# Windowed attention inside a hybrid encoder: the two halves of each P^T V product issued as a pair, transposes ordered by key block over two K heads, a fourth P^T buffer

## The chip, the cores and the metric

One core of a Trainium2 chip runs the whole program. The metric is device time in microseconds (us) of one execution; the median of several executions is compared.

## The reference

A trunk of two layers runs over two sequences, one of 2048 and one of 256 tokens, with 1024 features: first a windowed attention layer, then a bidirectional mLSTM layer, each with RMS norm, a gate, an output projection and a residual. The change touches the attention layer alone. Its core is:

```python
s = jnp.einsum('bnqgrd,bnkgd->bngrqk', qb, kb, preferred_element_type=jnp.float32)
s = s * (ATTN_HEAD_DIM ** -0.5)
...
s = jnp.where(mask[None, :, None, None], s, -jnp.inf)
...
m = jnp.maximum(jnp.max(s, axis=-1, keepdims=True), sk)
p = jnp.exp(s - m)
den = jnp.sum(p, axis=-1, keepdims=True) + jnp.exp(sk - m)
p = (p / den).astype(vb.dtype)
o = jnp.einsum('bngrqk,bnkgd->bnqgrd', p, vb).reshape(B, S, ATTN_WIDTH)
```

There are 16 query heads in 4 groups of 4, one K head (64 wide) to a group. A block of 128 queries looks at its own block of 128 keys and at its two neighbours.

## The kernel before

The tokens are 18 tiles of 128: tiles 0 to 15 are the long sequence, 16 and 17 the short one. `attn_core` (line 394) goes through them. For tile t:

- `front(t + 2)` projects two tiles ahead: three outputs of 512 columns (K and V, and two halves of Q), each 24 products on PE at lines 376 to 378 (`pj`), since an fp32 operand is split into a high and a low part and three of the four cross products are taken. Rotations run on DVE, then `pk` and `pqt` transposes on PE (lines 433, 451), then casts to `KH`, `KL`, `Q` on ACT and DVE (lines 435, 436, 454 to 457).
- `scores()` takes the K heads g = 0 to 3 in turn. For each of the 4 query heads of g, two products of 384 columns on PE fill a PSUM tile `s` (lines 500, 501), and DVE adds the mask into an SBUF tile `Sm` with the row maximum on the side (line 503). Then DVE makes `nm` and `es` (lines 508, 510) and ACT takes four exponentials in place (line 514). There are 11 buffers for `Sm` (`NSM`), four of them taken by each K head.
- `transposes()` turns the probabilities over. For one K head and one key block j, four PE transposes (line 528) fill a PSUM tile `ptp` (two buffers), and a copy (line 531) takes it to an SBUF tile `PT`: on ACT for j = 0, on DVE for the others. There are 3 buffers for `PT` (`NPT`). K heads go one after the other, each through all its key blocks.
- `values()` takes K heads in pairs P = 0, 1. One PSUM tile `o` (one buffer) holds both heads of a pair, the even one in partitions 0 to 63, the odd one in 64 to 127. For each key block and each of the two heads, one product (line 541, 128 x 64 weights of V, 512 columns of `PT`) adds into its half. An ACT copy (line 544) then takes `o` to `scr`, and a DMA stores it.

A tile at the edge of a sequence (0, 15, 16, 17) has two key blocks, the others three. So there are 800 transposes and 200 products of P^T with V. In the trace each of these products stands as two rows, for it passes its columns twice: 400 rows of line 541.

The order on the engines is set by the framework: the program is recorded with the generators interleaved by the string `AORDER` (f, s, p, v: a step of front, scores, transposes, values), and a scheduler with its own timeline then fixes the order of the instructions on each engine. A buffer is given when its last reader is done. Each engine then runs its list strictly in that order.

After attention come the gate product (`attn_gate`, whose weights `w_z` are loaded and split on ACT and DVE during the last tiles), the output projection and the mLSTM layer; the change does not touch them.

Of the kernel before, what the change touches and what calls it, by code (L numbers as in the profile page):

```python
# [11 lines left out]
F32 = mybir.dt.float32  # L12
# [13 lines left out]
HEADS, KVH, HD = 16, 4, 64  # L26
# [14 lines left out]
WOPS = ("b11", "t2", "b21", "t3", "t1", "t4", "b22")  # L41
PAIRS = [(t, t + 1) for t in range(0, NT, 2)]
NSM = 11
NPT = 3
SPT = 18
AORDER = "fffssssfsffffppsvppv"
AORDER1 = "fffssssfsffffppsvppv"
# [8 lines left out]
def seg_of(t):  # L56
    for s in SEGS:
        if s[0] <= t < s[1]:
            return s


class Trunk:
# [330 lines left out]
    def attn_core(self):  # L393
        nc, tc, a = self.nc, self.tc, self.a
        with ExitStack() as st:
            pe = st.enter_context(tc.tile_pool(name="a1e", bufs=2, reuse_waits="tile"))
            p = st.enter_context(tc.tile_pool(name="a1", bufs=2, reuse_waits="tile"))
# [67 lines left out]
            def half(t, h):  # L465
                X[t] += self.split(self.stage(a["xT"][t][:, h * 512:(h + 1) * 512]), nc.gpsimd if h else nc.vector)
# [12 lines left out]
            def core(t):  # L479
                s0, s1 = seg_of(t)  # L480
                kbs = [b for b in (t - 1, t, t + 1) if s0 <= b < s1]
                sl = sorted(b % 3 for b in kbs)
                vof = {b % 3: Vr[b] for b in kbs}
                nk = len(sl)
                step = sl[1] - sl[0]
                win = slice(sl[0], sl[-1] + 1, step)
                Ss, PTs = {}, {}

                def scores():
                    for g in range(KVH):  # L490
                        mx = p.tile([128, 4], F32, tag="mx", name="mx", bufs=3)
                        Sg = []
                        for c in range(GRP):
                            h = g * GRP + c
                            Q = QS[t, h // 8]
                            q = Q[:, h % 2, (h % 8) // 2, :]
                            spare = NT - 2 <= t < SPT and c % 3 == 2
                            S = (pq if spare else ps).tile([128, 3, 128], F32, tag="tq" if spare else "s", name="s",
                                                           bufs=1 if spare else 2)
                            nc.tensor.matmul(S[:, :nk, :], q, KH[:, g, win, :], start=True, stop=False)  # L500
                            nc.tensor.matmul(S[:, :nk, :], q, KL[:, g, win, :], start=False, stop=True)  # L501
                            Sm = p.tile([128, 3, 128], F32, tag="Sm", name="Sm", bufs=NSM)
                            nc.vector.tensor_tensor_reduce(Sm[:, :nk], S[:, :nk], mask[:, t % 3, win, :], 1.0, MASKED,  # L503
                                                           ALU.add, ALU.max, mx[:, c:c + 1])
                            Sg.append(Sm)
                        hs = slice(g * GRP, (g + 1) * GRP)
                        nm = p.tile([128, 4], F32, tag="nm", name="nm", bufs=3)
                        nc.vector.scalar_tensor_tensor(nm[:], mx[:], -HD ** -0.5, nsink[:, hs], ALU.mult, ALU.min)  # L508
                        es = p.tile([128, 4], F32, tag="es", name="es", bufs=3)
                        nc.vector.tensor_add(es[:], sink[:, hs], nm[:])  # L510
                        nc.scalar.activation(es[:], es[:], AF.Exp)
                        rs = p.tile([128, 4], F32, tag="rs", name="rs", bufs=3)
                        for c in range(GRP):
                            nc.scalar.activation(Sg[c][:, :nk], Sg[c][:, :nk], AF.Exp, bias=nm[:, c:c + 1],  # L514
                                                 scale=HD ** -0.5, accum_out=rs[:, c:c + 1])
                        Ss[g] = Sg
                        yield

                        nc.vector.tensor_add(rs[:], rs[:], es[:])
                        nc.vector.reciprocal(self.den[:, t, g // 2, :, g % 2], rs[:])  # L520

                def transposes():
                    for g in range(KVH):
                        PTs[g] = []
                        for j in range(nk):
                            tp = ps.tile([128, 4, 128], F32, tag="tr", name="ptp", bufs=2)
                            for c in range(GRP):
                                nc.tensor.transpose(tp[:, c, :], Ss[g][c][:, j, :], self.ident[:])  # L528
                            pt = p.tile([128, 512], F32, tag="PT", name="PT", bufs=NPT)
                            eng = nc.scalar.copy if j == 0 else nc.vector.tensor_copy  # L530
                            eng(pt[:], tp[:].rearrange("p c q -> p (c q)"))  # L531
                            PTs[g].append(pt)
                        yield

                def values():
                    for P in range(2):
                        o = ps.tile([128, 512], F32, tag="o", name="o", bufs=1)
                        for j in range(nk):
                            for gg in range(2):
                                g = 2 * P + gg  # L540
                                nc.tensor.matmul(o[gg * 64:(gg + 1) * 64, :], vof[sl[j]][:, g * HD:(g + 1) * HD],  # L541
                                                 PTs[g][j][:], start=j == 0, stop=j == nk - 1)
                        ob = self.scr[:, P * 512:(P + 1) * 512]
                        nc.scalar.copy(ob, o[:])
                        nc.sync.dma_start(self.oT[t][:, P * 512:(P + 1) * 512], ob)
                        yield

                return scores(), transposes(), values()

            def front(t):  # L550
# [555 lines left out]
```

## Time and profile before

| | |
|---|---|
| median of 3 runs | 2333.14 us (2330.55 to 2336.04) |
| profiled execution, its own time | 2326.69 us |
| span of its trace | 2324.8 us |
| TensorE's granted clock, mean over the span | 0.984 |
| PE busy | 2239.7 us, 96% |
| DVE busy | 1564.6 us, 67% |
| ACT busy | 1096.1 us, 47% |
| line 541, products of P^T with V | x400, busy 148.0 us together |
| line 528, transposes to `ptp` | x800, busy 127.9 us together |

PE is the matmul engine, PEld its weight loads, DVE the vector engine, ACT the scalar engine. Times of day in the trace count from the start of the span. A busy time is the union of the instructions in a group, and a mean is the length of one; since matmuls are pipelined, one that follows another starts before the first has ended, so what an instruction costs is read from one start to the next. PEclk is the granted share of the full 2.4 GHz. Attention's tiles run from about 60 to 712 us.

### The profile page before, as it was taken

What the parts mean: (1) busy time and instruction counts of PE and PEld (TensorE: products, weight loads), DVE (VectorE), ACT (ScalarE), POOL (GpSimd) and SP (SyncE); (2) the same over time, 40 slices, a digit from 0 to 9 for tenths busy, and PEclk for the clock granted to TensorE, in tenths of its full rate; (3) what the DMA queues carried; (4) which work ended last, traced back from release to release, by engine and by line L of the source; (5) the groups of instructions that cost most, each with busy time, mean ns of one, the idle gap of its engine ahead of it and who ended that gap; (6) DMA issues with size and microseconds to landing.
All of it is one profiled execution on the core that took longest, in us unless ns stands there. A gap on an engine that the chain in (4) does not pass through costs nothing.

```text
span 2324.8 us, 32958 instructions
## 1 busy us (share of the span) xinstructions
PE 2239.7 (96%) x11102; PEld 1775.3 (76%) x11102; DVE 1564.6 (67%) x3403; ACT 1096.1 (47%) x2503; POOL 461.4 (20%) x392
## 2 busy tenths in 40 slices
PE   8999999999999998999899999999999996999998
PEld 7766666666666886888788899978877875888887
DVE  7575656565877779768655522397888786777784
ACT  6464545454765334445533411256454445554463
POOL 3212121212001221322000000012242234333320
PEclk9999999999999999999999999999999997999999
DMA  7111111111225447657533722354565457656642
GB/s 264 48 38 48 38 48 38 48 38 39 91 64 162 147 159 229 230 195 250 189 114 123 245 92 92 113 177 136 175 211 182 132 181 242 207 191 198 209 163 69
DMA packets 170281, 326.41 MB, mean 140 GB/s; under 512 B 18784, under 2 KB 21632, under 8 KB 170112
## 3 DMA queue, kind: packets, MB, share of 16 engines
q1 hardware_dynamic: 169968, 324.30, 42.0%
q8 instruction: 88, 1.44, 0.3%
q14 instruction: 81, 0.66, 0.1%
q10 hardware_dynamic: 144, 0.01, 0.0%
HBM read 235.34 MB, written 88.89 MB: 139 GB/s over the span
## 4 chain that ended last, share of the span: by engine, by line
PE 78%; DVE 8%; DMA 7%; issue 2%; ACT 2%; POOL 2%; SPq 0%; DVEq 0%; POOLq 0%; ACTq 0%
PE pj L378 9%; PE pj L376 9%; PE pj L377 9%; PE o L541 5%; PE pj L271 4%; PE pj L272 4%; PE pj L273 4%; PE ptp L528 4%; PE d L271 3%; PE d L272 3%; PE d L273 3%; PE c L272 3%; PE c L273 3%; PE c L271 3%; DMA qs<-rows 2%
## 5 line engine op out<-in xcount | busy, mean ns | idle before, releaser
L122 ACT CAST xhi<-rawx 128x512 fp32r<-128x512 f32 x372 | 228.6, 618 | 459.6 <-PE pj L377 109.0
L376 PE MATMUL pj<-whi,xhi 128*128 128x512 f32 (+2 forms) x1152 | 429.9, 374 | 8.5 <-ACT whi L167 6.9
L378 PE MATMUL pj<-whi,xlo 128*128 128x512 f32 (+2 forms) x1152 | 423.8, 373 | 5.8 <-DVE xlo L123 3.9
L377 PE MATMUL pj<-wlo,xhi 128*128 128x512 f32 (+2 forms) x1152 | 425.4, 369 | 0.0
L123 DVE TENSOR_TENSOR xlo<-rawx,xhi 128x512 fp32r<-128x512 f32 x338 | 247.6, 737 | 81.7 <-ACT xhi L122 73.9
L378 PEld LDWEIGHTS pj<-whi,xlo 128*128 128x128 f32 x1152 | 217.3, 189 | 56.1 <-issue 14.6
L376 PEld LDWEIGHTS pj<-whi,xhi 128*128 128x128 f32 x1152 | 217.4, 189 | 48.5 <-ACT whi L167 7.3
L377 PEld LDWEIGHTS pj<-wlo,xhi 128*128 128x128 f32 x1152 | 217.4, 189 | 37.4 <-issue 3.2
L271 PE MATMUL pj<-whi,xhi 128*128 128x512 f32 x480 | 194.3, 405 | 13.9 <-DVE x L612 8.9
L503 DVE CUSTOM_DVE_ANT_0 Sm<-s,mask 128x384 f32<-128x384 f32 (+1 forms) x272 | 137.7, 529 | 92.0 <-PE s L501 90.9
L514 ACT ACTIVATE Sm<-Sm,nm 128x384 f32<-128x384 f32 (+1 forms) x288 | 166.9, 581 | 68.2 <-DVE nm L508 67.0
L272 PE MATMUL pj<-wlo,xhi 128*128 128x512 f32 x480 | 192.7, 401 | 2.9 <-DVE wlo L190 2.9
L273 PE MATMUL pj<-whi,xlo 128*128 128x512 f32 x480 | 191.8, 400 | 0.0
L541 PE MATMUL o<-PT,V 128*64 128x512 f32 x400 | 148.0, 623 | 4.5 <-DVE PT L531 4.1
L528 PEld LDWEIGHTS ptp<-ident,Sm 128*128 128x128 f32 x800 | 94.3, 141 | 64.8 <-issue 31.2
L531 DVE COPY PT<-ptp 128x512 f32<-128x512 f32 x128 | 86.6, 686 | 71.8 <-PE ptp L528 37.7
L528 PE MATMUL ptp<-ident,Sm 128*128 128x128 f32 x800 | 127.9, 280 | 4.1 <-ACT Sm L514 1.7
L271 PE MATMUL d<-whi,xhi 128*128 128x512 f32 x320 | 128.1, 400 | 0.0
L272 PE MATMUL c<-wlo,xhi 128*128 128x512 f32 x320 | 127.2, 398 | 0.0
L273 PE MATMUL c<-whi,xlo 128*128 128x512 f32 x320 | 127.1, 397 | 0.0
L273 PE MATMUL d<-whi,xlo 128*128 128x512 f32 x320 | 127.0, 397 | 0.0
L271 PE MATMUL c<-whi,xhi 128*128 128x512 f32 x320 | 127.0, 397 | 0.0
(243 smaller groups left out, 4714.1 us busy)
## 6 DMA issues: line engine op xcount, KB each, us to landing
rawx<-xn2T SPq DMA_DIRECT2D x144, 256.0 KB, 3.1
x<-x SPq DMA_DIRECT2D x108, 256.0 KB, 3.8
rawx<-xT SPq DMA_DIRECT2D x72, 256.0 KB, 2.9
raww<-w_oz SPq DMA_DIRECT2D x64, 256.0 KB, 4.4
raww<-w_qkvg SPq DMA_DIRECT2D x40, 256.0 KB, 4.0
v<-v SPq DMA_DIRECT2D x18, 516.0 KB, 3.7
rawx<-v SPq DMA_DIRECT2D x36, 258.0 KB, 2.7
rawx<-x SPq DMA_DIRECT2D x36, 256.0 KB, 3.0
```

What stands on the lines that cost most here:

```text
L122: nc.scalar.copy(hi[:], src)
L123: (eng or nc.vector).tensor_sub(lo[:], src, hi[:].bitcast(F32))
L271: nc.tensor.matmul(o, xh, wh, start=i == 0 and not more, stop=False, skip_group_check=more)
L272: nc.tensor.matmul(o, xh, wl, start=False, stop=False, skip_group_check=more)
L273: nc.tensor.matmul(o, xl, wh, start=False, stop=i == 3, skip_group_check=more)
L376: nc.tensor.matmul(o[:, :n], xh, wh, start=kt == 0, stop=False)
L377: nc.tensor.matmul(o[:, :n], xh, wl, start=False, stop=False)
L378: nc.tensor.matmul(o[:, :n], xl, wh, start=False, stop=kt == KT - 1)
L503: nc.vector.tensor_tensor_reduce(Sm[:, :nk], S[:, :nk], mask[:, t % 3, win, :], 1.0, MASKED, ALU.add, ALU.max, mx[:, c:c + 1])
L514: nc.scalar.activation(Sg[c][:, :nk], Sg[c][:, :nk], AF.Exp, bias=nm[:, c:c + 1], scale=HD ** -0.5, accum_out=rs[:, c:c + 1])
L528: nc.tensor.transpose(tp[:, c, :], Ss[g][c][:, j, :], self.ident[:])
L541: nc.tensor.matmul(o[gg * 64:(gg + 1) * 64, :], vof[sl[j]][:, g * HD:(g + 1) * HD], PTs[g][j][:], start=j == 0, stop=j == nk - 1)
```

## The change

`transposes()` now goes pair by pair, key block by key block, and within a key block over both K heads; it yields after the first and after the last key block of a pair. There are four `PT` buffers in place of three. `values()` issues the odd head's product of a key block first and places the even head's right behind it in PE's order: `tc.issue_after` puts the instructions recorded inside it directly behind the one named. No instruction is added or removed.

```diff
-NPT = 3
+NPT = 4
...
                 def transposes():
-                    for g in range(KVH):
-                        PTs[g] = []
-                        for j in range(nk):
+                    for P, j in product(range(2), range(nk)):
+                        for g in (2 * P, 2 * P + 1):
                             tp = ps.tile([128, 4, 128], F32, tag="tr", name="ptp", bufs=2)
                             for c in range(GRP):
                                 nc.tensor.transpose(tp[:, c, :], Ss[g][c][:, j, :], self.ident[:])
-                            pt = p.tile([128, 512], F32, tag="PT", name="PT", bufs=NPT)
+                            pt = PTs[g, j] = p.tile([128, 512], F32, tag="PT", name="PT", bufs=NPT)
                             eng = nc.scalar.copy if j == 0 else nc.vector.tensor_copy
                             eng(pt[:], tp[:].rearrange("p c q -> p (c q)"))
-                            PTs[g].append(pt)
-                        yield
+                        if j in (0, nk - 1):
+                            yield
 
                 def values():
                     for P in range(2):
                         o = ps.tile([128, 512], F32, tag="o", name="o", bufs=1)
+                        def half(j, gg):
+                            g = 2 * P + gg
+                            return nc.tensor.matmul(o[gg * 64:(gg + 1) * 64, :], vof[sl[j]][:, g * HD:(g + 1) * HD],
+                                                    PTs[g, j][:], start=j == 0, stop=j == nk - 1)
+
                         for j in range(nk):
-                            for gg in range(2):
-                                g = 2 * P + gg
-                                nc.tensor.matmul(o[gg * 64:(gg + 1) * 64, :], vof[sl[j]][:, g * HD:(g + 1) * HD],
-                                                 PTs[g][j][:], start=j == 0, stop=j == nk - 1)
+
+                            with tc.issue_after(half(j, 1).ins):
+                                half(j, 0)
```

What the scheduler makes of it is seen in the order of the instructions. Numbers tell apart tiles of one name. In the rows below `o_2150` and `o_2201` are the outputs of tile 2's first and second pair of K heads, and `Sm_1985` to `Sm_2000` are the probabilities of its last K head.

**First place: PE, tile 2, the products of its second pair.** Before, from the middle of it (the product of `PT_2164`, the even head's first key block, stands alone ahead of these rows):

```order
L541 MATMUL o_2201<-PT_2185,V_1254 64x512
L541 MATMUL o_2201<-PT_2171,V_1633 64x512
L500 MATMUL s_2295<-KH_283,Q_1684 128x384
L501 MATMUL s_2295<-KL_284,Q_1684 128x384
L500 MATMUL s_2300<-KH_283,Q_1684 128x384
L501 MATMUL s_2300<-KL_284,Q_1684 128x384
L541 MATMUL o_2201<-PT_2192,V_1633 64x512
L541 MATMUL o_2201<-PT_2178,V_907 64x512
L528 MATMUL ptp_2487<-ident_60,Sm_2265 128x128
L528 MATMUL ptp_2487<-ident_60,Sm_2270 128x128
L528 MATMUL ptp_2487<-ident_60,Sm_2275 128x128
L541 MATMUL o_2201<-PT_2199,V_907 64x512
```

Now, the end of the same products:

```order
L539 MATMUL o_2201<-PT_2171,V_1254 64x512
L539 MATMUL o_2201<-PT_2164,V_1254 64x512
L451 MATMUL pqt_2098<-ident_60,t1_2093 128x128 x4
L527 MATMUL ptp_2194<-ident_60,Sm_1985 128x128
L527 MATMUL ptp_2194<-ident_60,Sm_1990 128x128
L527 MATMUL ptp_2194<-ident_60,Sm_1995 128x128
L527 MATMUL ptp_2194<-ident_60,Sm_2000 128x128
L539 MATMUL o_2201<-PT_2185,V_1633 64x512
L539 MATMUL o_2201<-PT_2178,V_1633 64x512
L500 MATMUL s_2300<-KH_283,Q_1684 128x384
L501 MATMUL s_2300<-KL_284,Q_1684 128x384
L500 MATMUL s_2305<-KH_283,Q_1684 128x384
```

Before, the six products of the pair stood as one alone, two together (the odd head's of a key block and the even head's of the next), two together, one alone; now as three times two. Over the program the 200 products stood in 133 such groups (70 of one, 60 of two, 2 of three, 1 of four) and now stand in 99 (98 of two, 1 of four).

**Second place: PE, tile 2, the last score of the last K head** (`s_1997`, which fills `Sm_2000`). Before:

```order
L500 MATMUL s_1997<-KH_283,Q_1345 128x384
L501 MATMUL s_1997<-KL_284,Q_1345 128x384
L377 MATMUL pj_2407<-wlo_394,xhi_2212 128x512
L378 MATMUL pj_2407<-whi_395,xlo_2213 128x512
L376 MATMUL pj_2407<-whi_401,xhi_2212 128x512
L377 MATMUL pj_2407<-wlo_400,xhi_2212 128x512
L378 MATMUL pj_2407<-whi_401,xlo_2213 128x512
L376 MATMUL pj_2407<-whi_407,xhi_2212 128x512
L377 MATMUL pj_2407<-wlo_406,xhi_2212 128x512
L541 MATMUL o_2150<-PT_2141,V_1633 64x512
L541 MATMUL o_2150<-PT_2127,V_907 64x512
```

Now:

```order
L500 MATMUL s_1997<-KH_283,Q_1345 128x384
L501 MATMUL s_1997<-KL_284,Q_1345 128x384
L539 MATMUL o_2150<-PT_2148,V_907 64x512
L539 MATMUL o_2150<-PT_2141,V_907 64x512
L500 MATMUL s_2262<-KH_283,Q_1684 128x384
L500 MATMUL s_2267<-KH_283,Q_1684 128x384
L451 MATMUL pqt_2058<-ident_60,t1_2053 128x128 x4
L501 MATMUL s_2262<-KL_284,Q_1684 128x384
L501 MATMUL s_2267<-KL_284,Q_1684 128x384
L527 MATMUL ptp_2166<-ident_60,Sm_1985 128x128
L527 MATMUL ptp_2173<-ident_60,Sm_1952 128x128
```

The score now comes behind the last transposes of the first pair and right ahead of its last products; the first transpose that needs its K head's probabilities follows ten instructions later, where before the first pair's last two groups of products, projections and transposes of another head lay between. From `s_1997`'s second product to the first product of the second pair (`PT_2171`) PE now has: the second product itself, one pair of products, 10 more score products, 4 `pqt` transposes and 16 `ptp` transposes.

**Third place: ACT, tile 2, the copy of the odd head's first key block of the second pair.** Before (there it is `PT_2185`):

```order
L514 ACTIVATE Sm_2000,rs_2007<-Sm_2000,nm_2002 128x384
L544 COPY scr_70<-o_2150 128x512
L531 COPY PT_2164<-ptp_2159 128x512
L454 CAST Q_2063<-pqt_2058 64x512
L455 CAST Q_2063<-pqt_2058 64x512
L531 COPY PT_2185<-ptp_2180 128x512
```

Now (there it is `PT_2171`):

```order
L511 ACTIVATE es_2004<-es_2004 128x4
L514 ACTIVATE Sm_2000,rs_2007<-Sm_2000,nm_2002 128x384
L454 CAST Q_2063<-pqt_2058 64x512
L455 CAST Q_2063<-pqt_2058 64x512
L530 COPY PT_2171<-ptp_2166 128x512
```

The two casts still stand between the last exponential and this copy; what moved is the copy of `o` and that of the even head, which now come earlier in ACT's list.

## Rows read from the trace of the kernel before

**Rows 1.** Busy time by stretch of attention: start and end in us, length, then per engine the busy us and the count of instructions; PEclk is TensorE's granted clock, then the DMA engines' share and GB/s.
```profile
60.00:100.00 40.00, 40.00 (x198) 29.48 (x197) 22.37 (x66) 20.74 (x61) 12.04 (x10) 1.00 0.18 61
100.00:600.00 500.00, 496.64 (x2424) 342.35 (x2423) 307.55 (x911) 248.59 (x693) 85.16 (x74) 1.00 0.12 40
600.00:650.00 50.00, 47.97 (x235) 33.77 (x234) 47.89 (x123) 38.42 (x90) 5.56 (x4) 0.97 0.39 125
650.00:720.00 70.00, 62.92 (x284) 39.70 (x283) 46.81 (x159) 45.27 (x132) 4.17 (x3) 0.93 0.27 86
```

**Rows 2.** What PE waited for between 100 and 600 us: waiting instruction, releaser, us in total, times, longest.
```profile
PE o L541 <- DVE PT L531: 2.7, 5, 0.6
```

**Rows 3.** From the costliest groups of the page, the products of P^T with V: count, busy us together, mean ns of one, then PE's idle time just before them and what ended it.
```profile
L541 PE MATMUL o<-PT,V 128*64 128x512 f32 x400 | 148.0, 623 | 4.5 <-DVE PT L531 4.1
```

**Rows 4.** PE in order of time around tile 2's second pair: start, length, line, names, count, and in brackets an idle time ahead of it. A product with V is two rows of line 541, so "x2" is one product and "x4" two together.
```profile
200.23 1.07 PE L541 MATMUL o<-PT,V 128*64 128x512 f32 x2
201.23 0.44 PE L500 MATMUL s<-KH,Q 128*128 128x384 f32 x1
201.51 0.33 PE L501 MATMUL s<-KL,Q 128*128 128x384 f32 x1
201.68 0.34 PE L500 MATMUL s<-KH,Q 128*128 128x384 f32 x1
201.86 0.34 PE L501 MATMUL s<-KL,Q 128*128 128x384 f32 x1
202.04 0.60 PE L451 MATMUL pqt<-ident,t 128*128 128x128 f32 x4
202.47 1.04 PE L528 MATMUL ptp<-ident,Sm 128*128 128x128 f32 x8
203.44 1.08 PE L541 MATMUL o<-PT,V 128*64 128x512 f32 x4
204.45 0.44 PE L500 MATMUL s<-KH,Q 128*128 128x384 f32 x1
...
207.51 1.07 PE L541 MATMUL o<-PT,V 128*64 128x512 f32 x2 [0.59 <-DVE PT L531]
```

**Rows 5.** PE in order of time somewhat later, columns as in rows 4: projections, four transposes, two products together, a projection.
```profile
219.93 0.39 PE L377 MATMUL pj<-wlo,xhi 128*128 128x512 f32 x1
220.16 0.40 PE L378 MATMUL pj<-whi,xlo 128*128 128x512 f32 x1
...
224.33 0.60 PE L528 MATMUL ptp<-ident,Sm 128*128 128x128 f32 x4
224.86 1.08 PE L541 MATMUL o<-PT,V 128*64 128x512 f32 x4
225.87 0.50 PE L378 MATMUL pj<-whi,xlo 128*128 128x512 f32 x1
226.21 0.34 PE L500 MATMUL s<-KH,Q 128*128 128x384 f32 x1
```

**Rows 6.** Weight loads (PEld) in order of time, the ones of the two products together at 203.44.
```profile
203.44 0.20 PEld L541 LDWEIGHTS o<-PT,V 128*64 128x64 f32 x4 [0.17 <-issue]
```

**Rows 7.** PE in order of time: the second product of tile 2's last score.
```profile
189.39 0.34 PE L501 MATMUL s<-KL,Q 128*128 128x384 f32 x1
```

**Rows 8.** DVE in order of time, from that score's mask and maximum to `nm`.
```profile
189.77 0.56 DVE L503 CUSTOM_DVE_ANT_0 Sm<-s,mask 128x384 f32<-128x384 f32 x1
190.25 0.08 DVE L503 DVE_READ_ACCUMULATOR2_ANT mx<- 128x1 f32 x1
190.25 0.69 DVE L436 TENSOR_TENSOR KL<-pk,KH 128x512 fp32r<-128x512 f32 x1
190.85 0.15 DVE L508 SCALAR_TENSOR_TENSOR nm<-mx,nsink 128x4 f32<-128x4 f32 x1
```

**Rows 9.** ACT in order of time: the first exponential behind that `nm`; a copy to `PT`; two casts of `Q`; then from another tile the first of four exponentials and the instruction behind the fourth.
```profile
191.04 0.62 ACT L514 ACTIVATE Sm<-Sm,nm 128x384 f32<-128x384 f32 x1 [0.86 <-DVE nm L508]
...
194.14 0.59 ACT L531 COPY PT<-ptp 128x512 f32<-128x512 f32 x1
196.31 0.58 ACT L454 CAST Q<-pqt 64x512 fp32r<-64x512 f32 x1 [1.57 <-PE pqt L451]
196.90 0.58 ACT L455 CAST Q<-pqt 64x512 fp32r<-64x512 f32 x1
...
263.21 0.62 ACT L514 ACTIVATE Sm<-Sm,nm 128x384 f32<-128x384 f32 x1 [3.94 <-DVE nm L508]
...
265.71 0.56 ACT L531 COPY PT<-ptp 128x512 f32<-128x512 f32 x1
```

**Rows 10.** DVE in order of time, ahead of the product at 207.51.
```profile
205.34 0.69 DVE L456 TENSOR_TENSOR Q<-pqt,Q 64x512 fp32r<-64x512 f32 x1
206.04 0.69 DVE L457 TENSOR_TENSOR Q<-pqt,Q 64x512 fp32r<-64x512 f32 x1
206.76 0.69 DVE L531 COPY PT<-ptp 128x512 f32<-128x512 f32 x1
```

**Rows 11.** What PE waited for between 600 and 712 us, the three longest; columns as in rows 2.
```profile
PE s L500 <- DVE Q L457: 2.8, 1, 2.8
PE ptp L528 <- ACT Sm L514: 1.7, 2, 1.5
PE o L541 <- DVE PT L531: 1.4, 2, 1.3
```

**Rows 12.** Busy time between 672 and 684 us, columns as in rows 1.
```profile
672.00:684.00 12.00, 8.77 (x41) 7.42 (x42) 7.25 (x36) 7.64 (x27) 0.00 (x0) 0.72 0.06 23
```

## The prediction

> **What bounds the kernel now.** I read the busy times by stretch first. From 60 to 100 us PE is busy all the time, and from 100 to 600 us it is busy 496.64 of 500 us, while DVE has 307.55 and ACT 248.59 [rows 1]. So in tiles 0 to 14, where two tiles ahead are still being projected, the attention stage is as long as PE's list: a microsecond taken from that list is one from the time. The waits say the same: in these 500 us PE stood for products with V 2.7 us, five times [rows 2]. After 600 us it is different: DVE is busy 47.89 of 50 us, and up to 720 us PE idles 9 us, with single waits of up to 2.8 us for DVE and ACT [rows 1, 11]. There PE's time counts only in part.
>
> Then I read what a product with V costs. One alone starts at 200.23, and the next instruction starts at 201.23: 1.00 us. Two together, an odd head's and an even head's, run from 203.44 to 204.45: 1.01 us [rows 4]. The two write different halves of `o`'s partitions, use different halves of the array's columns, and pass side by side. So the second of a pair is free, and what counts is **slots**: a slot is one product alone or two together. In the 133 groups of the old order there are 136 or 137 (70 alone, 60 pairs, two slots in each of the 2 triples, two or three in the group of four). The trace agrees with 137: 137 x 1.08 us, the length of a slot, is 148.0 us, the busy time of the line [rows 3, 4].
>
> **The change, part by part.** *Slots.* In the new order 200 products stand as 98 pairs and one group of four: 100 slots, 37 fewer, and 34 groups fewer. Price of a slot that stands as its own group: 1.00 us, and a penalty on each side. Four transposes ahead of a product take 224.33 to 224.86, 0.53 us, where four ahead of other transposes take 202.04 to 202.47, 0.43: 0.10. Behind it the first score takes 201.23 to 201.51, 0.28, where the next takes 0.17; the first projection takes 225.87 to 226.21, 0.34, where one takes 219.93 to 220.16, 0.23: 0.11 each [rows 4, 5]. I take 1.2 us. Tiles 1 to 14 have 28 K-head pairs, each with 4 groups before and 3 now: 28 x 1.2 = 33.6 us, in the stretch where PE is the bound. Tile 0 loses a group and a slot inside a group: 1.2 + 1.0 = 2.2. Tiles 15 to 17 lose 5 groups and 2 slots inside groups: 5 x 1.2 + 2 x 1.0 = 8.0; there PE is not always the bound, so between 0 and 8.0, and I take half, 4.0.
>
> A rule of the Trainium skill speaks against all of this. The page "TensorE: Matmul & The Clock Gate" (Part 3: Packing small matmuls, The mechanism) says that a weight load overlaps a running matmul only when its row group differs; here both heads use all 128 rows, so the odd head's weights would have to be in before the even head's may load, and a pair would take two slots. Here the four weight loads of a pair stand within 0.20 us [rows 6] and the pair takes 1.01 us. The measurement decides, and the rule becomes a rival below.
>
> *Transposes in another order.* The same 800, with the same copies, 72 on ACT and 128 on DVE. Their count on PE does not change; I cost the order alone at nothing. What it changes is when things are ready, which is the next term.
>
> *New waits.* This is the cost. A pair of products needs both heads' transposes, so a pair's eight `Sm` buffers are held until its last key block is transposed, and of the 11 only 3 are left for the next pair's second head. Its fourth score (`s_1997` in the second order place) therefore comes late, just ahead of the first pair's last products. From there to the next pair's first product there is a chain on three engines, which I put together from rows. The score's second product starts at 189.39, its mask at 189.77, `KL` at 190.25, `nm` at 190.85, the exponential at 191.04: 1.65 us [rows 7 to 9]. Four exponentials with the small one among them take 263.21 to 265.71: 2.50 us [rows 9]. Two casts of `Q` stand ahead of the copy on ACT, 0.6 us each by their starts: 1.2. The copy takes 0.59 [rows 9], and I add 0.05 for its release. Sum 6.0 us. Meanwhile PE has (last rows of the second order place) one score product of 0.18, one pair with its penalties, 1.2, ten score products of 0.175 and twenty transposes of 0.11 [rows 4]: 5.3 us. So PE waits some 0.65 us in each tile's second pair. First pairs have projections in between and are covered. 14 tiles x 0.65 = 9 us. The lower end is no wait at all, and even the 2.7 us of old waits gone [rows 2], since the product at 207.51 which waited 0.59 us no longer stands alone. The upper end: two `Q` subtractions of 0.69 us ahead of a `PT` copy on DVE, as at 205.34 and 206.04 [rows 10], on top of the 0.65 in each tile: 14 x 2.05 = 29 us. I take 9, nearest to the chain as it stands in the new order.
>
> *Fourth `PT` buffer.* With three, the even head's copies filled all of them, and its first product had to go alone. With four, a key block of both heads is copied while another is used. Its gain is in the slots. Its room is in SBUF, with no instruction.
>
> *Queues.* Loads of `x` and stores of `o` change places with each other by a few rows in SP's list. The DMA engines are busy 0.12 of the time there [rows 1], which covers that; without the cover, one load late by a few us would show as a wait on `rawx` in the front, two tiles before it is needed.
>
> *Sum.* 33.6 + 2.2 + 4.0 - 9 = 31 us. The profiled execution took 2326.69 us, so it would be 2296; the median of the runs shown stands 6.4 us higher, 2333.14, and there the forecast is **2302 us**. The order of the later stages on PE changes at two or three places only, so I carry the gain through to the end.
>
> **The rivals.** *One, the waits eat most of it.* The upper ends together: 33.6 + 2.2 + 0 - 29 = 7 us of gain, 2326; with half of that wait, 2314. For it: ACT's list puts two casts ahead of the copy that PE needs. Against: before, the same casts stood there too, and PE waited 2.7 us in 500.
>
> *Two, slower: the fourth score's wait for its buffer.* The chain of 6.0 us starts when the first pair's last transposes release `Sm`. If those transposes are themselves late, since their copies wait for products that wait for the chain before, projections no longer cover first pairs either, and the wait comes twice a tile. It decides from 39.8 / 28 = 1.4 us of wait in each K-head pair. At the upper end of 2.05 us it would be 28 x 2.05 = 57 us against 39.8 gained: 17 us slower, 2350. Against it: PE's list still has the projections to fill first pairs.
>
> *Three, the pairs do not overlap.* If the second product of a pair has to wait until the first is through, every product is a slot: 200 in place of 137, at 1.0 us 63 us slower, 2396. (By the Trainium skill's rule quoted above it would.) In the trace the pairs that overlap are an odd head's product followed by an even head's, the order that the new code issues, so I give it next to nothing.
>
> *Four, nothing moves.* The 31 us would need 31 us of new waits to vanish within 4.7 us.
>
> **How the numbers follow.** Forecast 78%, rival one 12%, two 5%, three 1%, four 4%. The low end is all slots, the tail's too, with no new wait and the old ones gone: 33.6 + 2.2 + 8.0 + 2.7 = 46.5, 2287. That needs everything at once, so I put the low end at 2289. The high end takes in rival one past its half, at 2319. Within 0.2%, 4.7 us, a measurement of this kernel cannot tell a change from none. Faster by more than that: the forecast and rival one, 90%; within it 4%; slower 6%.
>
> **What would show it.** Right: line 541 (now 539) busy near 100 x 1.08 = 108 us in place of 148; rows of it "x4" with the next instruction 1.01 us later; attention's end some 30 us before its 712 us of now; new waits of about half a microsecond in each tile at the products with V, released by `PT` copies on ACT; later stages as long as before. Wrong: PE's idle time between 100 and 570 us over 15 us, or more than one such wait in a tile, or pairs of 2 us. In the tail a wait of 2.8 us was followed by a stretch at a granted clock of 0.72 [rows 11, 12]; a second such dip there would cost some 3 us and would say that the half taken for the tail was too much.

## The result, and the profile after

The median is **2318.13 us** (2316.6 to 2320.59, 4 runs), against 2332.64 us of the kernel before on the same chips (2330.55 to 2336.04, 4 runs): a ratio of 0.9937, 95% interval 0.992 to 0.9955. The change gains 14.5 us. Forecast were 31, and the median lies just inside the range, at its slow end.

The profiled execution after took 2317.46 us, close to its median, while the one of before stood 6 us below its own; so the two traces differ by 9.2 us only (2326.69 - 2317.46), and it is these that have to be explained from rows. One correction first: the tile that the sections above call tile 2 (its first pair of K heads ends at 193.66 us) is the fourth, tile 3 when counted from 0. The rows and the order are of the same tile, so no sum changes. Below it is called tile 3.

From the page of the kernel after, busy times and the chain that ended last, in shares of the span:

```profile
PE 2217.4 (96%) x11102; PEld 1763.2 (76%) x11102; DVE 1560.6 (67%) x3403; ACT 1095.8 (47%) x2503; POOL 464.7 (20%) x392
...
PE 74%; DVE 10%; DMA 7%; ACT 5%; issue 3%; POOL 2%; SPq 0%; DVEq 0%; POOLq 0%; ACTq 0%
```

Busy time by stretch, the answer to [rows 1]:

```profile
60.00:100.00 40.00, 40.00 (x210) 31.27 (x210) 24.26 (x74) 20.32 (x60) 12.66 (x11) 1.00 0.21 63
100.00:600.00 500.00, 487.89 (x2449) 338.92 (x2446) 307.24 (x917) 254.68 (x701) 87.57 (x74) 1.00 0.13 41
600.00:650.00 50.00, 44.42 (x225) 30.52 (x224) 45.74 (x112) 33.76 (x84) 4.21 (x3) 1.00 0.39 124
650.00:720.00 70.00, 63.14 (x308) 41.40 (x307) 50.52 (x165) 47.80 (x137) 5.05 (x4) 0.93 0.34 112
```

PE's idle time between 100 and 600 us rose from 3.4 to 12.1 us. What ended it, the answer to [rows 2], and the products with V between 60 and 715 us, the answer to [rows 3]:

```profile
PE ptp L527 <- DVE PT L530: 3.5, 11, 0.3
PE s L500 <- DVE mx L503: 3.3, 17, 0.2
PE s L500 <- ACT KH L435: 2.5, 5, 0.9
PE pqt L451 <- DVE nm L508: 0.7, 3, 0.2
```

```profile
L539 PE MATMUL o<-PT,V 128*64 128x512 f32 x400 | 109.7, 627 | 1.3 <-DVE PT L530 1.2
```

The products are what was forecast: 109.7 us busy, near 100 x 1.08. The waits are not. There is not one of a product with V in these 500 us. Transposes stand for a `ptp` buffer that a copy on DVE has to empty, and scores for an `s` buffer that a mask on DVE has to empty.

**Why idle time is not enough.** The copy of `o` to `scr` at the end of a pair marks the tiles. These are the copies of the first pair in tile 3 and in tile 15, and the last one of all, first before, then after (ACT in order of time):

```profile
193.66 0.59 ACT L544 COPY scr<-o 128x512 f32<-128x512 f32 x1
...
661.65 0.59 ACT L544 COPY scr<-o 128x512 f32<-128x512 f32 x1 [0.55 <-PE o L541]
...
711.94 0.59 ACT L544 COPY scr<-o 128x512 f32<-128x512 f32 x1 [4.69 <-PE o L541]
```

```profile
194.12 0.59 ACT L547 COPY scr<-o 128x512 f32<-128x512 f32 x1 [0.60 <-PE o L539]
...
656.33 0.56 ACT L547 COPY scr<-o 128x512 f32<-128x512 f32 x1
...
701.47 0.59 ACT L547 COPY scr<-o 128x512 f32<-128x512 f32 x1 [2.02 <-PE o L539]
```

Twelve tiles took 467.99 us and now take 462.21: 39.00 and 38.52 a tile, **0.48 us less in each**. By the slots it should have been 2 x 1.2 = 2.4 us less. So 1.9 us a tile went into waiting, three times the 0.65 forecast, though the idle time that the trace shows grew by 8.7 us in 500, which is some 0.7 a tile. The rest is hidden in the rows: they overlap. Transposes in a row start 109 ns apart and stand as 270 ns long, so one that starts 0.15 us late leaves no gap between two rows. From tile 15's first pair to the end it was 50.29 us and is 45.14: 5.2 us less. Up to tile 15 the gain is 5.3 us, at the end 10.5.

The 2.4 us can be measured too, from the start of one PE instruction to the start of the next. For each succession of two kinds (a transpose behind a transpose, a score behind a transpose, and so on) the median step between 100 and 600 us, over the traces of all fourteen kernels of this study, is taken as its cost, with the steps inside a slot and those from its first pass to its second kept apart. These costs added up are called PE's **list**, and what the steps are longer than that is called its **waits**. Over the same twelve tiles the list falls from 37.18 to 34.69 us a tile, 2.5 less, and the waits rise from 1.83 to 3.84, 2.0 more. So the slots gave what was forecast, and the waits took most of it. Scores wait 1.1 us a tile more, transposes to `ptp` 0.6, projections 0.4, `pqt` transposes 0.2; products with V wait 0.2 less. All of the 2.0 us stands where more than 4 us pass between two projections: 1.25 before, 3.21 after.

Where they are lost is seen in tile 3. PE in order of time, from the last score of the last K head (192.55) to the second pair's second group of products, the answer to [rows 4]:

```profile
192.55 0.34 PE L500 MATMUL s<-KH,Q 128*128 128x384 f32 x1
192.73 0.33 PE L501 MATMUL s<-KL,Q 128*128 128x384 f32 x1
192.99 1.08 PE L539 MATMUL o<-PT,V 128*64 128x512 f32 x4
194.00 0.62 PE L500 MATMUL s<-KH,Q 128*128 128x384 f32 x2
...
195.36 0.93 PE L527 MATMUL ptp<-ident,Sm 128*128 128x128 f32 x6
...
196.84 0.27 PE L527 MATMUL ptp<-ident,Sm 128*128 128x128 f32 x1
197.30 0.44 PE L500 MATMUL s<-KH,Q 128*128 128x384 f32 x1 [0.20 <-DVE mx L503]
197.58 0.34 PE L501 MATMUL s<-KL,Q 128*128 128x384 f32 x1
197.76 0.27 PE L527 MATMUL ptp<-ident,Sm 128*128 128x128 f32 x1
198.33 1.25 PE L527 MATMUL ptp<-ident,Sm 128*128 128x128 f32 x8 [0.30 <-DVE PT L530]
199.51 1.08 PE L539 MATMUL o<-PT,V 128*64 128x512 f32 x4
200.52 0.66 PE L451 MATMUL pqt<-ident,t 128*128 128x128 f32 x4
201.01 0.60 PE L527 MATMUL ptp<-ident,Sm 128*128 128x128 f32 x4
201.54 1.08 PE L539 MATMUL o<-PT,V 128*64 128x512 f32 x4
```

From 192.73 to the product at 199.51 are 6.78 us, where PE's work was put at 5.3: 1.45 us lost, and the trace shows 0.50 us of idle in it. See the lone transposes at 196.84 and 197.76, each followed by something late. The pairs themselves take 1.01 us (199.51 to 200.52). DVE and ACT in the same stretch, a line each of what is waited for, and the `PT` copy on ACT that was forecast as the one that ends last:

```profile
196.68 0.56 DVE L503 CUSTOM_DVE_ANT_0 Sm<-s,mask 128x384 f32<-128x384 f32 x1 [0.36 <-PE s L501]
...
197.52 0.66 DVE L530 COPY PT<-ptp 128x512 f32<-128x512 f32 x1
```

```profile
194.60 0.62 ACT L514 ACTIVATE Sm<-Sm,nm 128x384 f32<-128x384 f32 x1
...
197.68 0.58 ACT L455 CAST Q<-pqt 64x512 fp32r<-64x512 f32 x1
198.29 0.59 ACT L530 COPY PT<-ptp 128x512 f32<-128x512 f32 x1
```

That copy is done at 198.88, before PE has come to its product. It is the stretch ahead of it that is slow: PE, DVE and ACT hand single tiles to each other with no projection in between (the next one on PE starts at 207.42). By the steps PE's list up to the product is 5.27 us, as forecast, with 1.5 us of waits; and from the product at 199.51 to the projection at 207.42 stand another 1.4 us of waits, which the prediction's sum did not look at. The chain that ended last says it in one line. By line, shares of the chain between 100 and 600 us, first before, then after:

```profile
by line: PE o L541 19.3%; PE pj L378 14.8%; PE pj L376 14.5%; PE pj L377 14.3%; PE ptp L528 14.3%; PE s L500 7.5%; PE s L501 6.7%; PE pqt L451 2.7%; DVE PT L531 1.8%; PE pk L433 1.0%; issue 0.6%; DVE Q L457 0.6%; DVE Q L456 0.5%; ACT Q L455
```

```profile
by line: PE pj L376 14.8%; PE pj L378 14.3%; PE pj L377 14.2%; PE ptp L527 13.0%; PE o L539 12.5%; PE s L500 5.4%; PE s L501 4.9%; ACT Sm L514 3.4%; PE pqt L451 2.7%; DVE Sm L503 2.6%; DVE PT L530 1.8%; issue 1.2%; PE pk L433 1.0%; ACT scr 
```

Added up, the PE entries that the lines show held 95.1% of the chain and now hold 82.8%, while PE is busy 97.6% of that time. A busy PE is no longer the only bound: exponentials (3.4%) and masks (2.6%) are links of the chain that before had no share worth a place in the line. In tile 3 it reads, through DVE ahead of the second pair's products and through ACT behind the first of them:

```profile
196.47 0.19 PE s L501
...
196.68 0.56 DVE Sm L503
...
197.61 0.59 DVE PT L530
...
198.33 1.25 PE ptp L527 x8
...
201.21 0.58 ACT Q L454
...
201.81 0.58 ACT Q L455
...
202.93 1.98 ACT Sm L514 x7
```

### The profile page after: what moved, and what is told of

Read it like the earlier page. It is cut to its first block, busy times and chain, and to the rows that moved or that the text cites. A ratio compares the mean times of both kernels' runs of the same rounds, so it can differ in the third digit from the quotient of the medians.

```text
span 2315.6 us, 32977 instructions
## 1 busy us (share of the span) xinstructions
PE 2217.4 (96%) x11102; PEld 1763.2 (76%) x11102; DVE 1560.6 (67%) x3403; ACT 1095.8 (47%) x2503; POOL 464.7 (20%) x392
## 4 chain that ended last, share of the span: by engine, by line
PE 74%; DVE 10%; DMA 7%; ACT 5%; issue 3%; POOL 2%; SPq 0%; DVEq 0%; POOLq 0%; ACTq 0%
PE pj L376 9%; PE pj L378 9%; PE pj L377 9%; PE pj L271 4%; PE pj L272 4%; PE pj L273 4%; PE ptp L527 3%; PE o L539 3%; PE d L271 3%; PE d L272 3%; PE d L273 3%; PE c L272 3%; PE c L273 3%; PE c L271 3%; DMA qs<-rows 2%
## 5 line engine op out<-in xcount | busy, mean ns | idle before, releaser
L376 PEld LDWEIGHTS pj<-whi,xhi 128*128 128x128 f32 x1152 | 217.4, 189 | 51.1 <-issue 8.8
L527 PE MATMUL ptp<-ident,Sm 128*128 128x128 f32 x800 | 135.3, 280 | 9.6 <-DVE PT L530 6.3
L272 PE MATMUL d<-wlo,xhi 128*128 128x512 f32 x320 | 127.1, 397 | 0.0
L271 PEld LDWEIGHTS pj<-whi,xhi 128*128 128x128 f32 x480 | 92.0, 192 | 37.2 <-ACT whi L189 12.4
```

Of the source, the lines that this page charges most:

```text
L271: nc.tensor.matmul(o, xh, wh, start=i == 0 and not more, stop=False, skip_group_check=more)
L272: nc.tensor.matmul(o, xh, wl, start=False, stop=False, skip_group_check=more)
L376: nc.tensor.matmul(o[:, :n], xh, wh, start=kt == 0, stop=False)
```

## The experiments

Two theories stood against each other. **The late score** (A1): what the slots gave was spent because a pair's eight `Sm` buffers are held, so that the last K head's scores come late, and the second pair then needs both heads' first key blocks at once; more `Sm` buffers give it back, in the new order alone. **DVE** (A3; A2 in the first expectations): in that stretch DVE has too much to do; less work on DVE gives it back, more `Sm` buffers do not. "us a tile" below is taken as above, between the first copies of `o` in tiles 3 and 15 of the profiled execution. Every ratio is against the kernel before on the same chip, so two kernels are compared by their ratios. List and waits are PE's, in us a tile, as defined above.

| kernel | median, us | ratio to before, 95% | us a tile | list | waits |
|---|---|---|---|---|---|
| before | 2329.74 to 2332.64 | 1 | 39.00 | 37.18 | 1.83 |
| after | 2318.13 | 0.9937, 0.992 to 0.9955 | 38.52 | 34.69 | 3.84 |
| e1: before, four `PT` | 2334.13 | 1.002, 1.001 to 1.003 | 39.77 | 36.94 | 2.84 |
| e2: after, head by head | 2297.80 | 0.9861, 0.9846 to 0.9876 | 36.94 | 34.48 | 2.47 |
| e3: after, not issued as pairs | 2380.86 | 1.0222, 1.0205 to 1.0239 | 41.72 | 38.96 | 2.76 |
| e9: after, 12 `Sm` | 2306.56 | 0.9889, 0.9868 to 0.9911 | 37.85 | 34.81 | 3.05 |
| e10: after, 13 `Sm` | 2302.39 | 0.988, 0.9853 to 0.9907 | 37.50 | 34.69 | 2.81 |
| e4: after, 14 `Sm` | 2292.36 | 0.9834, 0.9816 to 0.9852 | 37.13 | 34.71 | 2.41 |
| e6: e2 with 14 `Sm` | 2300.56 | 0.9868, 0.9855 to 0.988 | 37.06 | 34.94 | 2.12 |
| e5: before, 14 `Sm` | 2331.68 | 1.0001, 0.9991 to 1.001 | 39.10 | 37.18 | 1.94 |
| e11: before, 9 `Sm` | 2331.78 | 1.0004, 0.999 to 1.0019 | 38.92 | 36.59 | 2.34 |
| e7: after, no low part of Q | 2312.35 | 0.992, 0.9907 to 0.9933 | 38.24 | 34.44 | 3.81 |
| e8: before, no low part of Q | 2322.88 | 0.9971, 0.9958 to 0.9983 | 37.80 | 36.12 | 1.68 |
| e12: after, more copies on ACT | 2323.38 | 0.9969, 0.9953 to 0.9986 | 39.03 | 34.67 | 4.36 |

The marks do not enclose quite the same work. Between them stand 870 projection products before, 864 after, 871 in e4, 849 in e2 and 820 in e8, at 0.23 us each: for the work of before, e2 would stand near 37.3 us a tile and e8 near 38.8.

**The parts of the change, each alone.** The fourth buffer in the old order:

```diff
-NPT = 3
+NPT = 4
```

> The kernel before with four PT buffers in place of three and nothing else of the change. Its products still stand unpaired: 123 groups, 138 slots by the order (before: 137 slots). Theory A (the gain comes from the 37 slots, and part of it is lost to waits for DVE): no slot is saved, so 2333 us, within 5 us. Rival (the fourth buffer itself frees copies and transposes, and that is what was gained): near 2318.

It is 0.2% slower (1.001 to 1.003), not faster: the buffer gives nothing by itself. Next, after with the pairs and the four buffers, but the transposes head by head again:

```diff
-                    for P, j in product(range(2), range(nk)):
-                        for g in (2 * P, 2 * P + 1):
+                    for g in range(KVH):
+                        for j in range(nk):
...
-                        if j in (0, nk - 1):
-                            yield
+                        yield
```

> The changed kernel with the transposes head by head again, as before the change; pairs and four PT buffers stay. 101 slots in 87 groups by the order. The even head's Sm buffers are free again after its own three key blocks. Theory A1 (holding eight Sm buffers to the end of a pair makes the next head's last score late and bunches DVE's work): the waits of the changed kernel, some 2 us a tile, mostly go, 2295 to 2308 us. Theory A2 (DVE is the bound wherever PE has no projections, whatever the Sm buffers do): 2315 to 2322, as the changed kernel.

By the ratios (0.9861 against 0.9937) it is some 18 us faster than after. So of the three parts the order of the transposes is the one that costs, with 11 `Sm` buffers. Then after without the placing of the second product behind the first:

```diff
-                            with tc.issue_after(half(j, 1).ins):
-                                half(j, 0)
+                            half(j, 0)
+                            half(j, 1)
```

> The changed kernel without the placing of the even head's product right behind the odd head's: transposes by key block over both heads and four PT buffers stay, products are issued as the scheduler likes. 172 slots in 171 groups by the order, against 100 in 99. If PE's list were the bound everywhere: 72 slots at 1.2 us more than the changed kernel, 2318 + 86 = 2404. Theory A (DVE is the bound in about half of each tile, so slots there cost less): 2345 to 2375. Rival (pairing by the scheduler's order matters little, the time comes from DVE and ACT alone): under 2335.

Its products with V between 60 and 800 us:

```profile
L539 PE MATMUL o<-PT,V 128*64 128x512 f32 x400 | 184.6, 618 | 3.5 <-DVE PT L530 1.3 <-ACT PT L530 1.1
```

184.6 us are 172 slots of 1.07, and 72 slots more than after cost 62.7 us (2380.86 - 2318.13), 0.87 us a slot, or 66 us by the ratios. That lies between what was expected if PE's list were the bound everywhere (2404) and theory A (2345 to 2375). The table says why: the list is 4.3 us a tile longer, for 4 slots (1.07 each), and the waits 1.1 shorter. What a slot costs was right in kind, some 1.1 on PE, and less in time where waits stand.

**More `Sm` buffers, in both orders.**

```diff
-NSM = 11
+NSM = 14
```

> The changed kernel with 14 Sm buffers in place of 11; pairs and order of transposes stay, 100 slots in 99 groups. Theory A1 (the late fourth score, for want of an Sm buffer, bunches DVE's work): 2296 to 2310 us. Theory A2 (DVE is the bound wherever PE has no projections): 2314 to 2322, as the changed kernel.

This is the fastest kernel of the study, some 24 us faster than after by the ratios and 37 faster than before on its chip. PE in order of time around the same last products of tile 3's first pair (190.19 here), and the two marks:

```profile
189.86 0.40 PE L377 MATMUL pj<-wlo,xhi 128*128 128x512 f32 x1
190.19 1.08 PE L539 MATMUL o<-PT,V 128*64 128x512 f32 x4
191.20 0.66 PE L527 MATMUL ptp<-ident,Sm 128*128 128x128 f32 x4
191.62 0.48 PE L378 MATMUL pj<-whi,xlo 128*128 128x512 f32 x1
...
193.10 0.39 PE L378 MATMUL pj<-whi,xlo 128*128 128x512 f32 x1
193.33 0.34 PE L500 MATMUL s<-KH,Q 128*128 128x384 f32 x1
```

```profile
191.32 0.59 ACT L547 COPY scr<-o 128x512 f32<-128x512 f32 x1 [1.32 <-PE o L539]
...
636.83 0.57 ACT L547 COPY scr<-o 128x512 f32<-128x512 f32 x1
```

Seven projections stand on each side of these products; in after they end at 192.32, ahead of the last score, and the next comes at 207.42. In the order, the last score now stands 38 rows ahead of these products, where in after it is 2. The tile takes 37.13 us, 1.87 less than before: of the 2.4 us of the slots four fifths are back. The list is that of after, and the waits are 1.4 us less. The same buffers in the old order:

> The kernel before with 14 Sm buffers in place of 11, nothing of the change; 136 or 137 slots in 133 groups, as before. Theory A1 (only the new order, which holds eight Sm buffers to the end of a pair, runs short of them): no change, 2326 to 2334 us. Rival (more Sm buffers help whatever the order, and the 26 us of e4 are no part of the explanation): 2318 or less.

Nothing (1.0001). So it is not that the kernel wanted more `Sm` buffers: the new order does. And both remedies together:

> Pairs with transposes head by head and four PT buffers (as e2) and 14 Sm buffers (as e4). 106 slots in 93 groups by the order, against 101 in 87 for e2. Theory A1 (both remedies cure the same lack, the late fourth score): no better than e4 by more than the slots tell, 2290 to 2302. Rival (two separate causes): 2270 to 2285.

They don't add up: 2300.56, where e2 has 2297.8 and e4 2292.36 (its slots are 106 by the order, where those have 101 and 100). Both give back the same loss. Is it a threshold or a slope?

> The changed kernel with 12 Sm buffers. 102 slots in 100 groups. By the order, tile 2's last score s_1997 stands 17 rows ahead of the first pair's last products, where it stands 2 ahead with 11 buffers and 38 ahead with 14. Theory A1 (the later the last score, the more PE waits): between the changed kernel's 2318 and e4's 2292, at 2303 to 2313 us. Rival (one step: 14 buffers cure it, fewer do nothing): 2316 to 2322.

> The changed kernel with 13 Sm buffers. 101 slots in 100 groups; s_1997 stands 20 rows ahead of the first pair's last products by the order. Theory A1: a little better than 12 buffers, 2296 to 2308 us. Rival (one step at 14): 2316 to 2322.

With 11, 12, 13 and 14 buffers: 2318, 2307, 2302, 2292 us, and 38.52, 37.85, 37.50, 37.13 us a tile. It is no threshold at 14: the twelfth buffer and the fourteenth give some, while the step from 12 to 13 lies within the intervals. The score moves away from the products as they are added: in the order of tile 3 it stands 2, 17, 20 and 38 rows ahead of them. Three kinds of tile recur, and in the trace, for most of the twelve tiles, the rows between the two are 4, 16 and 22 in e9, 4, 16 and 39 in e10, 4, 45 and 64 in e4; in after there is none in two of the kinds, and in the third the score is behind the products.

**Is a late score enough?** The old order with so few buffers that its last score too comes late, 4 rows ahead of a product:

```diff
-NSM = 11
+NSM = 9
```

> The kernel before with 9 Sm buffers in place of 11; 136 slots in 124 groups. By the order s_1997 now stands 4 rows ahead of a product of the first pair's last key blocks, where it stood 9 ahead with 11. Theory A1 says that the old order runs short of buffers too once there are few enough, and that a late last score costs there as in the new one: 2336 to 2352 us. Rival (a late last score costs only because the new order has fewer slots to cover it): 2326 to 2334.

In time the late score alone costs nothing that shows (1.0004, 0.999 to 1.0019, so at most some 4 us), against what A1 expected. In the trace 2 rows lie between the score and the products in two of three tiles, and the score is behind them in the third, nearly as in after. Busy time of e11 in the same 500 us:

```profile
100.00:600.00 500.00, 495.73 (x2411) 340.45 (x2410) 288.78 (x906) 247.59 (x695) 84.22 (x73) 1.00 0.12 41
```

PE is busy 0.9 us less than in [rows 1]. The steps show more, 0.5 us of waits a tile above before. In the old order the even head's twelve transposes and its own products come before the odd head's first transpose, so the late head has that much time. It takes both, the score late and both heads' first key blocks wanted at once: the old order has waits of 1.8 us a tile, with a late score 2.3 (e11); the new order with the score early has 2.4 (e4), with the score late 3.8 (after). With the pairs but head by head, e6 has 2.1, though its score stands 3 rows and none ahead of the products in two of three tiles.

**Less work on DVE.** A3 had a ground. Busy time in tile 3's stretch without projections, columns as in [rows 1], first before, then after:

```profile
199.00:211.70 12.70, 12.03 (x61) 6.50 (x59) 8.33 (x25) 5.78 (x15) 0.32 (x1) 1.00 0.06 23
```

```profile
195.30:207.40 12.10, 11.30 (x59) 6.32 (x59) 11.41 (x36) 8.73 (x25) 0.00 (x0) 1.00 0.11 43
```

DVE is busy 8.33 us there before and 11.41 of 12.10 after. The two subtractions that make the low part of Q, 0.69 us each [rows 10], were taken out of after and of before:

```diff
-                nc.vector.tensor_sub(Q[64:128, 0], pt[0:64], Q[0:64, 0].bitcast(F32))
-                nc.vector.tensor_sub(Q[0:64, 1], pt[64:128], Q[64:128, 1].bitcast(F32))
+                nc.gpsimd.memset(Q[64:128, 0].bitcast(F32), 0.0)
+                nc.gpsimd.memset(Q[0:64, 1].bitcast(F32), 0.0)
```

> The changed kernel with the low part of Q left out: its two subtractions a Q half on DVE (4 of 0.69 us a tile) are replaced by zeros that POOL writes. 100 slots as in the changed kernel, Sm buffers 11. Theory A3 (PE's new waits are for DVE's amount of work in the stretch without projections): 2.8 us a tile less there gives back most of the lost 2 us a tile, 2290 to 2303 us. Rival A1 (the order: the last score starts a chain of DVE, ACT and PE steps too late, and its length counts): 2308 to 2318, since the subtractions stand on that chain only in part.

> The same replacement (low part of Q left out, zeros from POOL) in the kernel before. PE's list is the bound there and waits for DVE are 0.2 us a tile, so all theories say little change: 2320 to 2332 us. If it gains as much as e7 does against the changed kernel, DVE's subtractions cost the same in both and tell nothing of the new waits.

By the ratios after gains some 4 us by it (0.9937 to 0.992) and before some 7 (0.9971). If DVE's amount of work were what ate the slots, after would have to gain more than before. The waits of e7 are as long as those of after, 3.81 us a tile. They do change places, though: those of transposes to `ptp` fall from 1.2 to 0.5, and those of `pqt` transposes rise from 0.3 to 0.7, some of them behind the zeros on POOL. So the run is no clean test of DVE's share. Last, two more of a tile's twelve `PT` copies turned over from DVE to ACT, in after with its 11 `Sm` buffers (in spite of the label):

```diff
-                            eng = nc.scalar.copy if j == 0 else nc.vector.tensor_copy
+                            eng = nc.scalar.copy if j == 0 or (j == 1 and g % 2 == 0 and nk == 3) else nc.vector.tensor_copy
```

> The changed kernel, 11 Sm buffers, with the even head's copy of the middle key block on ACT in place of DVE: 28 copies of 0.69 us leave DVE, 28 of 0.59 us join ACT. 100 slots. Theory A3 (DVE's amount of work in the stretch without projections) says 1.4 us a tile less on DVE gives 2300 to 2310 us. Theory A1 (order, not amount): 2312 to 2322, as the changed kernel.

It is not faster than after: 0.9969 against 0.9937, and the two intervals just touch. A3 expected 2300 to 2310 us, and it took 2323.38. The wait for a `ptp` buffer has changed its engine and grown, from 3.5 to 11.3 us (PE's longest entry between 100 and 600 us):

```profile
PE ptp L527 <- ACT PT L530: 11.3, 13, 0.9
```

So less work on DVE does not give the slots back. Nor do e4's waits shrink because an engine is less full: where more than 4 us pass between projections, DVE is busy 83% of the time after and 89% in e4, ACT 71% and 70%, and the waits there are 3.2 us a tile after and 1.7 in e4. The links of the chain are on DVE and ACT; what fits these runs is that it is their length, begun late, that counts. That ACT's list, which e12 made longer, has no share in it is not shown: no run took work off ACT.

## Why the prediction was right and where it was wrong

*The slots: right.* 100 of them, 1.01 us a pair in the trace, the line's busy time 109.7 us for 108 forecast. Rival three falls with it. The sentence of the Trainium skill (the page "TensorE: Matmul & The Clock Gate", Part 3: Packing small matmuls, The mechanism) that a weight load overlaps running matmuls only when its row group differs does not describe this trace: both heads use the same rows, and the pair takes 1.01 us after as it did before. That a pair must then take two slots was the prediction's inference and not the page's. The price of 1.2 us holds: PE's list is 2.5 us shorter in each tile for the 2.4 forecast. e3 gives 0.87 us for a slot in time, with shorter waits mixed in, and e4 brings 1.87 of the 2.4 us of two slots in each tile.

*Transposes in another order at nothing but the wait: right in kind.* Their count and copies are the same, and e2 shows that most of the loss hangs on their order, with 11 `Sm` buffers: 1.4 of the 2.0 us of new waits a tile.

*The new waits: the step that failed.* Forecast were 0.65 us a tile, 9 in all, with 2.05 a tile, 29 in all, as the upper end. Measured from step to step are 2.0 us a tile, 28 us up to tile 15's first pair: the upper end. The mechanism was named: eight `Sm` buffers held, three left, the last score right ahead of the first pair's last products. Its size was taken as the difference of two sums up to one point, the first product of the second pair, as if PE's 5.3 us of work up to there ran on while the chain ran. It did not. PE's work there was sized rightly, 5.27 us by the steps, and it took 6.78. The rows show that the work which was to be the cover (ten score products, twenty transposes) waits itself: scores for `s` buffers that masks empty, transposes for `ptp` buffers that copies empty, each copy in DVE's list behind masks. PE was given cover that hung on the same two engines as the chain. And behind that product, where the sum ended, as much again was lost up to the next projection (1.4 us in tile 3). The projections, of which only the first behind a pause was seen to wait for DVE (0.6 us in 500), had gone elsewhere in PE's list. In the order they were seen to be missing there, and that was counted as less cover, not as a stretch in which nothing runs freely. So the releaser was wrong too: `PT` copies on ACT were forecast, and not one wait that the trace shows in 500 us was for them.

*The tail: near, and in part by luck.* 5.2 us less from tile 15's first pair on, for 4.0 taken as half of 8.0. But 2.3 of them are ten products of the gate stage that now stand ahead of that mark (48 in place of 38). PE's list gave 4.6 us more, and 2.0 went into new waits. The granted clock of the last 70 us is 0.93 as before.

*The sum, mended*, from step to step. Between 60 us and tile 15's first pair PE's list is 33.2 us shorter, and 35.5 without those ten products, where the slots were to give 33.6 + 2.2. Its waits are 28.1 longer, where 9 were forecast. That leaves some 5 us, and the tail some 5 more: with about 40 us of slots and 30 of waits the end of attention is 10.5 us earlier, as the last mark says, where some 30 were forecast. The later stages give 1.2 us back (from that mark to the end of the span 1612.9 and now 1614.1), which leaves the 9.2 us between the traces. The medians differ by 14.5; the 5.3 us between the two numbers are that the profiled execution of before stood 6 us below its median and that of after 0.7 below.

*Rival one is what happened*, at 12%: the waits eat most of it, between its half, 2314 (by its own terms 33.6 + 2.2 - 14.4 = 21.4 us of gain, so 2312), and its upper ends, 2326. Its ground was right in part: it named the casts ahead of a copy on ACT. Rival two, slower, would have needed the wait in both pairs of each tile; the first pairs kept their projections. Rival four, no change, falls with the ratio's interval.

*The marks set for right and wrong.* "PE's idle time over 15 us" between 100 and 570 us was to tell that the waits were mis-sized. It is 12.1 us between 100 and 600, and still they were: idle time was the wrong measure.

What stays open: which link of the tile's second pair holds each part of the 2.0 us. Every kernel here is scheduled anew, so its order differs in more places than the edit; no run moved the projections alone, and none took work off ACT.

## What to carry to other kernels

When a reorder holds a group of buffers for longer, ask which producer is now late, and then what the waiting engine has left to do that does not depend on the engines of that chain: work that does may wait along with the chain, so its microseconds are not all cover (here 5.3 us of it took 6.8). After a change that ought to shorten a busy engine's list, take the time between two marks of the loop, the steps from start to start and the engine's share of the chain of waits, not its idle time. When a reorder pays less than its count says, try one to three buffers more for what it now holds: here that turned 14.5 us into 37.

## What the runs showed that was not expected

Idle time in the trace leaves out most short waits of a pipelined engine: 1.9 us a tile by the marks and 2.0 by the steps, against some 0.7 of new idle rows. Transposes start 109 ns apart and stand as about 270 ns, the score products 176 ns apart and stand as 340, so a start that is 0.15 us late leaves no gap. And the same three buffers for `Sm` are worth some 24 us in one order and nothing (1.0001, 0.9991 to 1.001) in the other.
